# Attention scores of two heads issued in turns on the two halves of the rows, in a two-block sequence kernel on one Trainium2 core

## The chip, the cores and the metric

The kernel runs on one core of a Trainium2 chip. The metric is the time of one execution on the device in microseconds (us), as the median of several runs. The engines are named as the profile names them: PE is the matrix engine (TensorE) and PEld its weight loads, DVE is VectorE, ACT is ScalarE, POOL is GpSimd, SP is the engine that issues the loads from memory. PE writes its results into eight banks of PSUM, each of 128 partitions by 512 float32.

## What is computed

The reference is a chain of two blocks on 512 tokens of width 1024: a gated linear-attention layer, then a recurrent layer and an attention layer, each with feed-forward parts. The change lies in the attention layer alone, with 16 heads of width 64:

```python
def block(args):                       # one block of 128 queries
    qb, start = args
    z = jnp.einsum("bhqd,bhkd->bhqk", qb.astype(jnp.float32), k32) * scale
    q_pos = start + jnp.arange(Q_BLOCK)
    mask = key_pos[None, :] < q_pos[:, None]
    log_beta = jax.nn.log_sigmoid(z)
    log_1m = jnp.where(mask, jax.nn.log_sigmoid(-z), 0.0)
    suffix = lax.cumsum(log_1m, axis=3, reverse=True) - log_1m
    wts = jnp.where(mask, jnp.exp(log_beta + suffix), 0.0)
    return jnp.einsum("bhqk,bhkd->bhqd", wts, v32)
...
qkv = (h @ w_qkv.astype(h.dtype)).reshape(bsz, s, 3, SB_HEADS, SB_HEAD_DIM)
...
return o @ w_out.astype(h.dtype)
```

## The kernel before

All matrices are kept transposed (features on the partitions, tokens along the row). A float32 product is made of three products of rounded parts: every operand is split into a high and a low part (`...h`, `...l`), by a cast on ACT and a subtraction on DVE. Weights come from memory in slabs of 128 columns (`raw`), one load from SP each. `Feed` keeps the list of slabs in the order of their use; it splits each two products ahead (`whi`, L101 on ACT; `wlo`, L102 on DVE) into one of three slots.

The attention layer goes through eight passes `k`, each with two heads: head a lies on partitions 0 to 63 of the pass's q and k tiles, head b on partitions 64 to 127. The order of PE's instructions is the order in which the code is written (`manual_schedule`); those of the other engines are ordered by the framework. A pass has these steps:

- `proj`: the projections q, k and v of 24 products of 512 columns each (`psmm`, L173 to L175; for v they are named `psv` and come in two halves of 12). `evac` scales and splits the result: for q it is `qh` and `ql`, for k and v first `qk` (L1172).
- `scores(half, ...)`, L1119: twelve products of one head that contract 64 rows (`z`). Their widths are three times 512, 384, 128 and 256, since each of the four query blocks needs only its own and earlier keys; they fill three banks z0, z1, z2. Each bank then goes through eight sigmoids in all on ACT (`om`, `be`, L1124), masks on POOL (L1128), a scan on DVE (`pr`, L1131) and a product on DVE (`be`, L1134).
- `turn`, L1146: ten transposes of the weights `be` into three banks (t0, t1 and `nr`), and their split into w0, w1 and w2 (L1103, L1104).
- `vparts`, L1182: four transposes of v (`pv`) and their split (`vh`, `vl`).
- `values`, L1157: twelve products with v (`po`) of the same widths as the scores, and the split of the result (`Oh`, `Ol`, L1161 and L1162), the input of the output projection (`pso`, `out_part`).

PSUM's banks are shared out as two for projections, v's transposes and `po` (`mm`), three for the scores, two for the transposes, and one (`nr`) for the third group of the transposes.

Before, PE does in a pass: scores of head b, turn of a, projection k of the next pass, values of a, half of projection v, scores of head a of the next pass, turn of b, the other half of projection v, projection q of the pass after the next, values of b, and the transposes of v. So the scores of the two heads stand half a pass apart.

## Time and profile before

| what | value |
|---|---|
| median of three runs | 2080.22 us (2080.13 to 2083.77) |
| the profiled execution | 2082.17 us |
| its span | 2080.2 us |
| PE's busy share of the span | 99% |
| DVE, ACT, POOL | 53%, 37%, 12% |
| the eight attention passes | some 200 us from 1451 us on |

The profiled execution is 1.95 us above the median, and 1.97 us of it lie outside the span. The trace gives each instruction with its start and length. PE's instructions overlap: the length of a product contains its way through the array, so the rate is read from the distance of two starts, not from the length. "Idle" in brackets behind an instruction is the time in which its engine stood still before it, with the engine and the line that ended the wait.

### The profile page before, as it was taken

What the parts mean: (1) busy time and instruction counts of PE and PEld (TensorE: products, weight loads), DVE (VectorE), ACT (ScalarE), POOL (GpSimd) and SP (SyncE); (2) the same over time, 40 slices, a digit from 0 to 9 for tenths busy, and PEclk for the clock granted to TensorE, in tenths of its full rate; (3) what the DMA queues carried; (4) which work ended last, traced back from release to release, by engine and by line L of the source; (5) the groups of instructions that cost most, each with busy time, mean ns of one, the idle gap of its engine ahead of it and who ended that gap; (6) DMA issues with size and microseconds to landing.
All of it is one profiled execution on the core that took longest, in us unless ns stands there. A gap on an engine that the chain in (4) does not pass through costs nothing.

```text
span 2080.2 us, 24373 instructions
## 1 busy us (share of the span) xinstructions
PE 2051.9 (99%) x9786; PEld 1705.2 (82%) x9786; DVE 1104.5 (53%) x1455; ACT 763.9 (37%) x1099; POOL 257.1 (12%) x266
## 2 busy tenths in 40 slices
PE   8999999999999999999899999999999999999998
PEld 7778899888888888887788888888888888888887
DVE  5667453554444423669964444333877754444322
ACT  4334232333232322546642323223555533322221
POOL 0111000131000000252320000001322220000011
PEclk9999999999999999999999999999999999999999
DMA  4211111343333333322323333333122123333332
GB/s 168 71 55 59 60 41 43 105 127 101 97 96 100 91 97 98 114 79 82 91 91 96 97 101 92 92 101 98 55 61 72 41 77 96 91 102 94 92 102 68
DMA packets 53664, 181.69 MB, mean 87 GB/s; under 512 B 5808, under 2 KB 7984, under 8 KB 53552
## 3 DMA queue, kind: packets, MB, share of 16 engines
q1 hardware_dynamic: 53408, 180.05, 28.9%
q8 instruction: 76, 1.25, 0.3%
q14 instruction: 36, 0.29, 0.0%
q10 hardware_dynamic: 144, 0.10, 0.0%
HBM read 178.03 MB, written 2.10 MB: 87 GB/s over the span
## 4 chain that ended last, share of the span: by engine, by line
PE 91%; DVE 5%; ACT 1%; issue 1%; POOL 1%; DMA 1%; SPq 0%; POOLq 0%; DVEq 0%; ACTq 0%
PE psmm L173 19%; PE psmm L174 19%; PE psmm L175 19%; PE psd L173 6%; PE psd L175 6%; PE psd L174 6%; PE z L1119 2%; PE po L1157 1%; DVE wlo L102 1%; PE pU L731 1%; PE pX L726 1%; PE t L1146 1%; DVE xc L987 1%; PE psv L173 1%; PE psv L174 1%
## 5 line engine op out<-in xcount | busy, mean ns | idle before, releaser
L101 ACT CAST whi<-raw 128x1024 fp32r<-128x1024 f32 (+1 forms) x333 | 344.5, 1036 | 942.3 <-issue 374.5
L102 DVE TENSOR_TENSOR wlo<-raw,whi 128x1024 fp32r<-128x1024 f32 (+1 forms) x333 | 411.0, 1235 | 287.9 <-ACT whi L101 287.8
L173 PE MATMUL psmm<-Bh,wlo 128*128 128x512 f32 x1032 | 402.3, 390 | 0.3 <-DVE Ol L1162 0.3
L174 PE MATMUL psmm<-Bl,whi 128*128 128x512 f32 x1032 | 402.2, 390 | 0.1
L175 PE MATMUL psmm<-Bh,whi 128*128 128x512 f32 x1032 | 402.1, 390 | 0.0
L173 PE MATMUL psmm<-Ah,wlo 128*128 128x512 f32 x832 | 332.9, 401 | 2.8 <-DVE wlo L102 1.9
L175 PE MATMUL psmm<-Ah,whi 128*128 128x512 f32 x832 | 325.2, 391 | 0.0
L174 PE MATMUL psmm<-Al,whi 128*128 128x512 f32 x832 | 324.4, 390 | 0.6 <-DVE Al L189 0.6
L173 PEld LDWEIGHTS psmm<-Bh,wlo 128*128 128x128 f32 x1032 | 193.8, 188 | 40.8 <-DVE Ol L1162 0.5
L175 PEld LDWEIGHTS psmm<-Bh,whi 128*128 128x128 f32 x1032 | 193.8, 188 | 40.3
L174 PEld LDWEIGHTS psmm<-Bl,whi 128*128 128x128 f32 x1032 | 193.8, 188 | 40.2 <-DVE Bl L189 0.5
L216 POOL TENSOR_TENSOR ss<-ss,sq 128x512 f32<-128x512 f32 x55 | 85.6, 1561 | 1141.7 <-issue 803.7
L173 PE MATMUL psd<-Hh,wlo 128*128 128x512 f32 x506 | 196.8, 389 | 0.0
L174 PE MATMUL psd<-Hl,whi 128*128 128x512 f32 x506 | 196.8, 389 | 0.0
L175 PE MATMUL psd<-Hh,whi 128*128 128x512 f32 x506 | 196.8, 389 | 0.0
L173 PEld LDWEIGHTS psmm<-Ah,wlo 128*128 128x128 f32 x832 | 156.3, 188 | 36.0 <-DVE wlo L102 3.2
L175 PEld LDWEIGHTS psmm<-Ah,whi 128*128 128x128 f32 x832 | 156.1, 188 | 33.6
L174 PEld LDWEIGHTS psmm<-Al,whi 128*128 128x128 f32 x832 | 156.6, 188 | 30.3 <-DVE Al L189 1.1
L870 DVE TENSOR_TENSOR u<-psmm,R 128x512 f32<-128x512 f32 x66 | 45.6, 691 | 194.2 <-PE psmm L175 194.2
L866 DVE TENSOR_TENSOR s<-psmm,R 128x512 f32<-128x512 f32 x66 | 45.7, 692 | 137.0 <-PE psmm L175 134.0
L175 PEld LDWEIGHTS psd<-Hh,whi 128*128 128x128 f32 x506 | 95.0, 188 | 19.8
L174 PEld LDWEIGHTS psd<-Hl,whi 128*128 128x128 f32 x506 | 95.0, 188 | 19.8
(468 smaller groups left out, 2475.9 us busy)
## 6 DMA issues: line engine op xcount, KB each, us to landing
raw<-in_f SPq DMA_DIRECT2D x120, 512.0 KB, 3.6
raw<-in_w SPq DMA_DIRECT2D x60, 512.0 KB, 3.5
raw<-in_wA SPq DMA_DIRECT2D x43, 512.0 KB, 3.5
raw<-in_bQKV SPq DMA_DIRECT2D x24, 512.0 KB, 3.5
raw<-in_aIn SPq DMA_DIRECT2D x16, 512.0 KB, 3.6
raw<-in_f SPq DMA_DIRECT2D x16, 384.0 KB, 3.1
x<-in_xT SPq DMA_DIRECT2D x16, 256.0 KB, 3.6
raw<-in_wBr SPq DMA_DIRECT2D x8, 512.0 KB, 3.5
```

The source lines that it names most:

```text
L101: copied[0] = S.copy(hi[:, :nk, :], raw[:, :nk, :])
L102: V.tensor_tensor(lo[:, :nk, :], raw[:, :nk, :], hi[:, :nk, :].bitcast(F32), op=ALU.subtract)
L173: TE.matmul(ps, l, xh, start=(first and i == 0), stop=False)
L174: TE.matmul(ps, h, xl, start=False, stop=False)
L175: TE.matmul(ps, h, xh, start=False, stop=(last and i == n - 1))
L216: eng.tensor_tensor(self.acc, self.acc, sq, op=ALU.add)
L726: heads(lambda h: TE.matmul(pX[:, h], Nm[:, h, :], odd(U)[:, h], start=True, stop=True))
L731: heads(lambda h: TE.matmul(pU[:, h], Tt[:, h, :], X[:, h], start=True, stop=True))
L866: V.tensor_tensor(s1, p1, R, op=ALU.mult)
L870: V.tensor_tensor(u, p3, R, op=ALU.mult)
L987: V.scalar_tensor_tensor(ac, cx[:, j:j + T], col("aconv", 4 * k + j), ac, op0=ALU.mult, op1=ALU.add)
L1119: TE.matmul(zs[g][:, o:o + w], qp[a][qs], kp[b][p0:p0 + 64, 0:w], start=(n == 0 and o == 0), stop=(n == 2), skip_group_check=True)
```

## The change

`scores` now makes the products of both heads in one call: for every product of head a the same of head b follows at once, into a bank of its own. The sigmoids, masks, scans and products that stood in `scores` are now in `mix`, called once for each head. Each head has three banks (z00, z01, z02 and z10, z11, `nr`); the transposes of a head go into the banks of its scores, and its products with v into the third of these, which holds only 256 columns of scores. The two `mm` banks are left to the projections and v's transposes. In a pass PE now does: scores of both heads, projections q and k of the next pass, turn of a, half of projection v, turn of b, the other half, values of a, transposes of v, values of b. Before the first pass, v's transposes stand ahead of the scores. The list of slabs follows: q, k, v for each pass. The tiles of q and k have one buffer instead of two, those of w0, w1 and w2 two instead of one.

```diff
--- before.py
+++ after.py
@@ -159,9 +159,8 @@
     feed.add([aO[m] for m in range(KD)])
     feed.mark((0, 0, 1))
     ffn_plan(f13[0], f2[0])
-    feed.add([bQKV[8], bQKV[9], bQKV[0], bQKV[10]])
-    for k in range(KD - 1):
-        feed.add([bQKV[9 + 2 * (k + 1)], bQKV[k + 1]] + ([bQKV[8 + 2 * (k + 2)]] if k < KD - 2 else []))
+    for k in range(KD):
+        feed.add([bQKV[8 + 2 * k], bQKV[9 + 2 * k], bQKV[k]])
     feed.mark((2, 0, 0, 1))
     feed.add([bO[m] for m in range(KD)])
     feed.mark((0, 0, 1))
@@ -1104,20 +1103,29 @@
             V.tensor_tensor(lo[:, 0:w], src, hi[:, 0:w].bitcast(F32), op=ALU.subtract)
             return hi, lo
 
-        def scores(half, qp, kp):
-
-            p0 = 64 * half
-            zs = [psz.tile([P, T], F32, tag=f"z{g}", name=f"z{g}") for g in range(3)]
+        def bank(half, g, name):
+            if half and g == 2:
+                return pn.tile([P, T], F32, tag="nr", name=name)
+            return psz.tile([P, T], F32, tag=f"z{half}{g}", name=name)
+
+        def scores(qp, kp):
+
+
+            zs = [[bank(half, g, f"z{g}") for g in range(3)] for half in range(2)]
+            for g, i, o, w in QB:
+                for n, (a, b) in enumerate(((0, 1), (1, 0), (0, 0))):
+                    for half in range(2):
+                        p0 = 64 * half
+                        TE.matmul(zs[half][g][:, o:o + w], qp[a][p0:p0 + 64, i * P:(i + 1) * P], kp[b][p0:p0 + 64, 0:w],
+                                  start=(n == 0 and o == 0), stop=(n == 2), skip_group_check=True)
+            return zs
+
+        def mix(zs):
             be = SB.tile([P, 1280], F32, tag="be", bufs=2, name="be")
             om = SB.tile([P, 1280], F32, tag="om", bufs=2, name="om")
             pr = SB.tile([P, 1280], F32, tag="pr", bufs=1, name="pr")
             for g in range(3):
                 qbs = [(i, o, w) for g_, i, o, w in QB if g_ == g]
-                for i, o, w in qbs:
-                    qs = slice(p0, p0 + 64), slice(i * P, (i + 1) * P)
-                    for n, (a, b) in enumerate(((0, 1), (1, 0), (0, 0))):
-                        TE.matmul(zs[g][:, o:o + w], qp[a][qs], kp[b][p0:p0 + 64, 0:w], start=(n == 0 and o == 0),
-                                  stop=(n == 2), skip_group_check=True)
                 c0, cw = ZW[g]
                 for t, n in ((om, 1), (be, 0)):
                     for i, o, w in qbs:
@@ -1134,21 +1142,20 @@
                 V.tensor_tensor(be[:, c0:c0 + cw - 1], be[:, c0:c0 + cw - 1], pr[:, c0 + 1:c0 + cw], op=ALU.mult)
             return be
 
-        def turn(be):
+        def turn(half, be):
 
             out = []
             for g, (w, js) in enumerate(ZG):
-                t = pn.tile([P, T], F32, tag="nr", name="t2") if g == 2 else psz.tile([P, T], F32, tag=f"t{g}", name=f"t{g}")
+                t = bank(half, g, f"t{g}")
                 for j in js:
                     for i in range(j, NB):
                         c = next(ZW[g_][0] + o for g_, i_, o, _ in QB if i_ == i) + j * P
                         o = ZP[j][1] + (i - j) * P
                         TE.transpose(t[:, o:o + P], be[:, c:c + P], ident)
-                out.append(parts(f"w{g}", t[:, 0:w], w, 1))
+                out.append(parts(f"w{g}", t[:, 0:w], w, 2))
             return out
 
-        def values(k, half, wts, vp, pool=pmm, tag="mm"):
-            po = pool.tile([P, T], F32, tag=tag, name="po")
+        def values(k, half, wts, vp, po):
             n = 0
             for g in range(3):
                 for j in ZG[g][1]:
@@ -1167,10 +1174,10 @@
         def evac(ps, w):
 
             if w == 0:
-                return parts("q", ps, T, 2)
+                return parts("q", ps, T, 1)
             t = tp.tile([P, T], F32, tag="xin", bufs=3, name="qk")
             V.tensor_tensor(t, ps, R, op=ALU.mult)
-            return t if w == 2 else parts("k", t, T, 2)
+            return t if w == 2 else parts("k", t, T, 1)
 
         def proj(k, w):
 
@@ -1192,44 +1199,41 @@
             mm3(ps, [(hi[:, c, :], lo[:, c, :], O[c]) for c in ks], first=ks[0] == 0, last=ks[-1] == KD - 1)
 
         with tc.manual_schedule(engines={mybir.EngineType.PE}):
-            q, kk = proj(0, 0), proj(0, 1)
-            vt = proj(0, 2)
-            wa = scores(0, q, kk)
-            qn = proj(1, 0)
+            q, kk, vt = proj(0, 0), proj(0, 1), proj(0, 2)
             v = vparts(vt)
             for k in range(KD):
-                more = k < KD - 1
-                wb = scores(1, q, kk)
-                wt = turn(wa)
-                if more:
-                    kk, q = proj(k + 1, 1), qn
-                    values(k, 0, wt, v)
+                za, zb = scores(q, kk)
+                wa = mix(za)
+                if k < KD - 1:
+                    q = proj(k + 1, 0)
+                    wb = mix(zb)
+                    kk = proj(k + 1, 1)
+                    ta = turn(0, wa)
                     vhi, vlo = feed.next(bQKV[k + 1])
                     pv = pmm.tile([P, T], F32, tag="mm", name="psv")
                     mm3(pv, [(vhi[:, c, :], vlo[:, c, :], A[c]) for c in range(4)], last=False)
-                    wa = scores(0, q, kk)
-                    wt = turn(wb)
+                    tb = turn(1, wb)
                     mm3(pv, [(vhi[:, c, :], vlo[:, c, :], A[c]) for c in range(4, 8)], first=False)
                     vt = evac(pv, 2)
-                    if k < KD - 2:
-                        qn = proj(k + 2, 0)
-                    else:
-                        out_part(0, range(0, 6))
-                    values(k, 1, wt, v)
-                    v = vparts(vt)
+                    values(k, 0, ta, v, bank(0, 2, "po"))
+                    vn = vparts(vt)
+                    values(k, 1, tb, v, bank(1, 2, "po"))
+                    v = vn
                 else:
+                    out_part(0, range(0, 7))
+                    wb = mix(zb)
                     out_part(1, range(0, 7))
-                    values(k, 0, wt, v, psz, "z0")
-                    out_part(0, range(6, 7))
-                    wt = turn(wb)
-                    out_part(2, range(0, 7), psz, "z1")
-                    values(k, 1, wt, v, psz, "z0")
-            out_part(3, range(0, 7), psz, "z2")
+                    ta = turn(0, wa)
+                    tb = turn(1, wb)
+                    out_part(2, range(0, 7), psz, "z00")
+                    values(k, 0, ta, v, bank(0, 2, "po"))
+                    values(k, 1, tb, v, bank(1, 2, "po"))
+            out_part(3, range(0, 7), psz, "z01")
             for m in range(4):
                 out_part(m, range(7, 8))
         ss = SumSq("ss7")
         for m in range(KD):
-            ps = part[m][2] if m in part else gemm(psz, bO[m], O, tag=("z0", "t0", "t1", "z1")[m % 4])
+            ps = part[m][2] if m in part else gemm(psz, bO[m], O, tag=("z10", "z11", "z02", "z00")[m % 4])
             V.tensor_tensor(x_tiles[m], ps, x_tiles[m], op=ALU.add)
             split_scaled(A[m], x_tiles[m], col("nf1", m))
             ss.add(x_tiles[m])
```

Where the instructions stand is shown at three places. The first is PE's row at the change from the second pass to the third, before (z0 and z1 are the first two banks of one head's scores, `kl`, `kh`, `ql`, `qh` the parts of k and q):

```order
L1182 MATMUL pv_11177<-CST_76,qk_11125 128x128 x4
L1119 MATMUL z0_11186<-kl_11007,qh_10876 128x512
L1119 MATMUL z0_11186<-kh_11006,ql_10877 128x512
L1119 MATMUL z0_11186<-kh_11006,qh_10876 128x512
L1119 MATMUL z1_11187<-kl_11007,qh_10876 128x384
L1119 MATMUL z1_11187<-kh_11006,ql_10877 128x384
L1119 MATMUL z1_11187<-kh_11006,qh_10876 128x384
L1119 MATMUL z1_11187<-kl_11007,qh_10876 128x128
```

and after, at the same place (z0_11107 belongs to head a, z0_11110 to head b):

```order
L1164 MATMUL po_11092<-w2l_11051,vh_10806 128x256
L1164 MATMUL po_11092<-w2h_11050,vh_10806 128x256
L1119 MATMUL z0_11107<-kl_10982,qh_10915 128x512
L1119 MATMUL z0_11110<-kl_10982,qh_10915 128x512
L1119 MATMUL z0_11107<-kh_10981,ql_10916 128x512
L1119 MATMUL z0_11110<-kh_10981,ql_10916 128x512
L1119 MATMUL z0_11107<-kh_10981,qh_10915 128x512
L1119 MATMUL z0_11110<-kh_10981,qh_10915 128x512
L1119 MATMUL z1_11108<-kl_10982,qh_10915 128x384
```

The second head's products, which stood after a turn, projections and values, now follow those of the first one by one, and `values` (`po`) instead of v's transposes stand ahead of them.

The second place is DVE's row in the pass, before, from the scan of a head's first bank to the evacuation of q (`ql`):

```order
L1131 SCALAR_TENSOR_TENSOR pr_10767<-om_10766,anew_10420 128x512
L1134 TENSOR_TENSOR be_10765<-be_10765,pr_10767 128x511
L1131 SCALAR_TENSOR_TENSOR pr_10767<-om_10766,anew_10420 128x512
L1134 TENSOR_TENSOR be_10765<-be_10765,pr_10767 128x511
L1131 SCALAR_TENSOR_TENSOR pr_10767<-om_10766,anew_10420 128x256
L1104 TENSOR_TENSOR w0l_10812<-t0_10806,w0h_10811 128x512
L1134 TENSOR_TENSOR be_10765<-be_10765,pr_10767 128x255
L1104 TENSOR_TENSOR w1l_10821<-t1_10815,w1h_10820 128x512
L1104 TENSOR_TENSOR w2l_10828<-t2_10824,w2h_10827 128x256
L1172 TENSOR_TENSOR qk_10843<-psv_10749,R6_10393 128x512
L102 TENSOR_TENSOR wlo_10848<-raw_10743,whi_10847 128x1024
L1104 TENSOR_TENSOR ql_10877<-psmm_10851,qh_10876 128x512
```

and after, from the scans of the second head on (head a's three scans and products stand right ahead of these):

```order
L1139 SCALAR_TENSOR_TENSOR pr_10921<-om_10920,anew_10420 128x512 x2
L1139 SCALAR_TENSOR_TENSOR pr_10921<-om_10920,anew_10420 128x256
L1142 TENSOR_TENSOR be_10919<-be_10919,pr_10921 128x511
L1103 TENSOR_TENSOR ql_10916<-psmm_10890,qh_10915 128x512
L1142 TENSOR_TENSOR be_10919<-be_10919,pr_10921 128x511
L1142 TENSOR_TENSOR be_10919<-be_10919,pr_10921 128x255
L102 TENSOR_TENSOR wlo_10951<-raw_10884,whi_10950 128x1024
L1179 TENSOR_TENSOR qk_10979<-psmm_10954,R6_10393 128x512
L102 TENSOR_TENSOR wlo_11013<-raw_10948,whi_11012 128x1024
L1103 TENSOR_TENSOR w0l_10991<-t0_10985,w0h_10990 128x512
```

The evacuation of q now stands behind the scans of both heads, ahead of the split of the transposes of head a (`w0l`).

The third place is PE's row right after the first projection of v, before (the last rows of that projection, then head a's scores):

```order
L174 MATMUL psmm_10507<-Bl7_6306,whi_10431 128x512
L175 MATMUL psmm_10507<-Bh7_6305,whi_10431 128x512
L1119 MATMUL z0_10534<-kl_10498,qh_10460 128x512
L1119 MATMUL z0_10534<-kh_10497,ql_10461 128x512
L1119 MATMUL z0_10534<-kh_10497,qh_10460 128x512
```

and after:

```order
L173 MATMUL psmm_10507<-Bl7_6306,whi_10431 128x512
L174 MATMUL psmm_10507<-Bh7_6305,whi_10431 128x512
L1189 MATMUL pv_10534<-CST_76,qk_10532 128x128 x4
L1119 MATMUL z0_10543<-kl_10498,qh_10460 128x512
L1119 MATMUL z0_10546<-kl_10498,qh_10460 128x512
```

The transposes of v stand directly behind v's projection now.

## Rows read from the trace of the kernel before

**Rows 1.** The page, part 1: busy time, share of the span, instructions of each engine.

```profile
PE 2051.9 (99%) x9786; PEld 1705.2 (82%) x9786; DVE 1104.5 (53%) x1455; ACT 763.9 (37%) x1099; POOL 257.1 (12%) x266
```

**Rows 2.** Busy time by stretch: one whole pass. Columns: length, engines, PEclk, DMA.

```profile
1486.80:1514.23 27.43, 27.43 (x145) 23.26 (x145) 21.41 (x29) 15.31 (x31) 7.83 (x12) 1.00 0.20 58
```

**Rows 3.** Timeline of PE, one scores call. Columns: start us, length us, instruction.

```profile
1486.80 0.50 PE L1119 MATMUL z<-kl,qh 64*128 64x512 f32 x1
1487.14 0.40 PE L1119 MATMUL z<-kh,ql 64*128 64x512 f32 x1
1487.38 0.39 PE L1119 MATMUL z<-kh,qh 64*128 64x512 f32 x1
...
1488.93 1.31 PE L1146 MATMUL t<-CST,be 128*128 128x128 f32 x10
```

**Rows 4.** Timeline of PE: first and last of twelve products with v.

```profile
1495.58 0.39 PE L1157 MATMUL po<-w0h,vl 128*128 128x512 f32 x1
...
1497.37 0.28 PE L1157 MATMUL po<-w2h,vh 128*128 128x256 f32 x1
```

**Rows 5.** Timeline of PE: a scores call between plain products.

```profile
1450.62 0.39 PE L174 MATMUL psmm<-Bl,whi 128*128 128x512 f32 x1
1450.85 0.39 PE L175 MATMUL psmm<-Bh,whi 128*128 128x512 f32 x1
1451.17 0.49 PE L1119 MATMUL z<-kl,qh 64*128 64x512 f32 x1
...
1453.28 0.50 PE L173 MATMUL psmm<-Bh,wlo 128*128 128x512 f32 x1
1453.62 0.40 PE L174 MATMUL psmm<-Bl,whi 128*128 128x512 f32 x1
```

**Rows 6.** Timeline of weight loads (PEld) in the scores call of rows 3.

```profile
1488.15 0.18 PEld L1119 LDWEIGHTS z<-kh,ql 64*128 64x128 f32 x1
1488.26 0.19 PEld L1119 LDWEIGHTS z<-kh,qh 64*128 64x128 f32 x1
1488.37 0.19 PEld L1119 LDWEIGHTS z<-kl,qh 64*128 64x128 f32 x1
```

**Rows 7.** Timeline of ACT: first sigmoid and first cast after one head's eight sigmoids.

```profile
1487.87 0.69 ACT L1124 ACTIVATE om<-z,rq 128x512 f32<-128x512 f32 x1 [0.21 <-PE z L1119]
...
1491.16 0.64 ACT L1103 CAST w0h<-t 128x512 fp32r<-128x512 f32 x1
```

**Rows 8.** Timeline of DVE: the scans and products of one head.

```profile
1488.95 1.22 DVE L1131 TENSOR_TENSOR_SCAN pr<-om,anew 128x512 f32<-128x512 f32 x1 [0.15 <-POOL om L1128]
1490.30 0.88 DVE L1134 TENSOR_TENSOR be<-be,pr 128x511 f32<-128x511 f32 x1
1491.10 1.42 DVE L1131 TENSOR_TENSOR_SCAN pr<-om,anew 128x512 f32<-128x512 f32 x1
1492.62 0.78 DVE L1134 TENSOR_TENSOR be<-be,pr 128x511 f32<-128x511 f32 x1
1493.32 0.68 DVE L1131 TENSOR_TENSOR_SCAN pr<-om,anew 128x256 f32<-128x256 f32 x1
...
1494.51 0.41 DVE L1134 TENSOR_TENSOR be<-be,pr 128x255 f32<-128x255 f32 x1
```

**Rows 9.** Timeline of PE: its two waits from the sixth pass on, idle time in brackets.

```profile
1627.94 0.50 PE L173 MATMUL psmm<-Bh,wlo 128*128 128x512 f32 x1 [0.30 <-DVE Ol L1162]
...
1652.57 0.66 PE L1182 MATMUL pv<-CST,qk 128*128 128x128 f32 x4 [1.40 <-DVE Ol L1162]
```

**Rows 10.** Busy time by stretch, columns as in rows 2: after two waits.

```profile
1654.00:1660.00 6.00, 6.00 (x24) 5.48 (x23) 4.66 (x5) 4.80 (x11) 3.64 (x6) 0.50 0.00 0
1036.00:1042.00 6.00, 5.19 (x23) 3.86 (x21) 5.86 (x4) 1.25 (x2) 4.15 (x3) 1.00 0.18 73
```

**Rows 11.** Timeline of PE: an earlier wait, for comparison.

```profile
1034.50 0.50 PE L173 MATMUL psmm<-Ah,wlo 128*128 128x512 f32 x1 [1.60 <-DVE wlo L102]
```

**Rows 12.** Timeline of DVE: the first evacuation of v's projection.

```profile
1451.27 0.69 DVE L1172 TENSOR_TENSOR qk<-psmm,R 128x512 f32<-128x512 f32 x1 [0.52 <-PE psmm L175]
```

## The prediction

> **What bounds the kernel now.** The page's first part says that PE is busy for 99% of the span [rows 1], so PE's own time decides, and other engines count only where PE waits for them. The second view is one attention pass by stretches: of its 27.43 us PE is busy for all, DVE for 21.41, ACT for 15.31, POOL for 7.83, at a granted clock of 1.00 [rows 2]. So a pass is a full row of PE, and DVE with 78% is the next. The third view, PE's timeline, gives the rate: a score product of 512 columns starts 0.24 us after the one ahead of it [rows 3], a plain one 0.23 [rows 5], though the first contracts 64 rows and the second 128. Half of the array's rows are unused, for the price of the whole. The fourth view is what PE waited for: in the last passes 0.30 and 1.40 us, both for the split of a finished `po` that still held one of the two `mm` banks [rows 9]. After the second the clock is at 0.50, the lower of the two levels, for 6 us [rows 10].
>
> **Scores in turns.** A call's twelve products take 2.13 us beside transposes [rows 3]. The twelve products with v have the same widths and take 1.92 (1497.37 - 1495.58 and 0.13 for the last) [rows 4]. So a call is 1.92 of products and 0.21 of edges, and a pass holds two: 3.84 without edges. Now pairs of products use different rows and different banks. If they run at once, what limits the pair? Each brings its own weight load, and loads follow each other at 0.11 us in the narrow products [rows 6]. 24 loads at 0.11 are 2.64 per pass, a gain of 1.20. This I take: it is the nearest row, and for pairs of 512 columns two loads (0.22) are no longer than one product. Ends: 1.92 per pass if loads of different rows also overlap (gain 1.92), 3.84 if the products do not (gain 0). No row shows two products on different halves side by side. Eight passes give 9.6 us, between 0 and 15.4.
>
> The Trainium skill, in "TensorE: Matmul & The Clock Gate", section "Measured speedup vs the span model", counts a group of row tiles as one matmul plus about 4 ns for each further tile; by that rule the term would be the upper end, 15.4. No run here shows it yet.
>
> **The edges.** A call between plain products costs 0.39 beyond its twelve (1453.62 - 1450.85 less two plain starts of 0.23 and 1.92) [rows 5], one beside transposes 0.21 [rows 3]. Now one call of the first kind replaces two calls that touch transposes on a side, and the transposes get edges of their own. I count this as even; ends are 0.2 per pass either way, 1.6 us in all.
>
> **The waits that go.** `po` no longer takes an `mm` bank, and no output projection holds one in the seventh pass. So the waits of 0.30 and 1.40 go [rows 9], and with the latter the stretch at half clock: 6 us at 0.50 lose 3.0 us [rows 10], 3.2 with its ends. That is 4.9 us. What would be late next there is v's evacuation, below. A fall of the clock does not follow each wait (after 1.60 us at 1034 it stayed at 1.00 [rows 10, 11]), so I bind it to no length.
>
> **The waits that come.** First, v's transposes now stand right behind its first projection. The evacuation ends at 1451.27 + 0.69 = 1451.96 [rows 12], where PE had its next row from 1451.08 [rows 5]: 1.0 us, once, behind it all scores. Second, in the last pass two output parts (21 products of 0.23 each) stand between the scores and the turns; the turn of b is then reached 13.6 us after the pass's start by the working below, and b's last product, with no `ql` ahead of it, ends at 14.6: 1.0 us, once. Together 2.0 us.
>
> **Does a pass keep its pace?** This is the working for the cover of the other engines, from the start of the scores, t = 0. PE: scores to 2.9 (2.64 and edges), projections q and k to 13.8 (48 at 0.23, rounded down), turn of a to 14.9 (ten transposes, 1.31 us with the way of the last through the array [rows 3], 1.1 by starts), half of v to 17.7, turn of b to 18.8, the rest to 21.6, values to 23.6, v's transposes to 24.1, values to 26.1. ACT: its sigmoids begin at 1.07 (1487.87 - 1486.80) and take 3.29 per head [rows 3, 7]; for both heads, bank by bank, they end near 7.8. POOL's twelve masks take 7.83 [rows 2] and end near 10.4. DVE: one head's scans and products take 6.0 from 2.15 on [rows 8]; with the masks of both heads interleaved, head a is done near 9.3, needed at 13.8. Head b follows: scans of 1.45, 1.45 and 0.65, a product of 0.8, and then `ql` (0.69, as long as the evacuation in [rows 12]; 0.6 by starts) end near 14.1; the products of 0.8 and 0.35 end near 15.3. `ql` frees the bank of `psv`, wanted at 14.9: 0.8 us to spare. Head b is wanted at 17.7: 2.4 to spare. Behind come the splits for the turns, `qk` of v near 22.6 (wanted at 23.6), `Ol` of b near 27.6 (its bank is wanted by the next pass at 28.2). So nothing waits, with 0.6 to 1.0 us to spare at three places. The moved slabs cost nothing: three loads, casts and `wlo` per pass as before, two products ahead. DVE would be busy for 21.4 of some 26.2 us.
>
> **The sum.** -9.6 - 4.9 + 2.0 = -12.5 us. Against the profiled execution's 2082.17 that is 2069.7; the median of the runs is 1.95 lower, so 2067.7.
>
> **Rivals.**
>
> *Loads overlap too.* A pair costs one product, 1.92 per pass. For it: the two heads use separate rows for weights as for data. Against: the 0.11 us between loads is seen even where nothing else is in the way [rows 6]. It gives 5.8 us more: 2061.9. It is the case of the skill's page named above.
>
> *Pairs do not overlap.* The change then does not do what it says; the order alone changes. For it: no row of this trace shows an overlap. Against: the pairs share neither rows nor banks. It gives 9.6 us less gain: 2077.3, within 0.2%.
>
> *DVE's row becomes the bound.* Head b's scans and `ql` come in one row ahead of `psv` on DVE, and POOL's masks feed them. If masks of two heads delay head a's scans by 2.2 us more than I worked out, `psv` waits 1.4 us in each of seven passes; a wait of this size has halved the clock once here [rows 9, 10], at 3.2 us. Seven times 4.6 are 32 us on 2067.7: 2100, slower. It decides from a delay of 0.8 us on; below some 2 us it only eats the gain (1 us of wait in seven passes: 2075). For it: little to spare, and masks whose length is read roughly. Against: head a has 4.5 us to spare, and only `ql` is tight.
>
> The skill warns of this in "TensorEngine Tiling (Array Packing)", section "PSUM Bottleneck": tiles speed up the products, not the emptying of PSUM, which may become the limit. Here ACT and DVE had 12 and 6 us free in a pass, and by that the rival stays small.
>
> **How the numbers follow.** I give the forecast 0.47, overlapping loads 0.18, no overlap 0.20, the bound on DVE with a falling clock 0.10, and short waits in each pass 0.05. A difference of 0.2% (4.2 us) is about what a measurement of this kernel can tell from none: faster is below 2076.0, slower above 2084.4. Faster holds the first two and half of the last, 0.68; within 0.2% are no overlap and the other half, 0.22; slower 0.10. The range runs from the case of overlapping loads with even edges (2062, and 2 us for the edges) to that of no overlap with worse edges: 2060 to 2079. It leaves out the case on DVE and a little beyond each end.
>
> **What would show it.** After: one call of 24 `z` products of about 3.0 us per pass, pairs of 512 columns starting 0.23 us apart by the pair, a pass of about 26.2 us, no wait of v's transposes for `Ol` and no stretch at 0.50 near the end, a wait of about 1 us of `pv` near 1451. Starts of `z` 0.2 us apart for every product would say that nothing overlaps; waits of `psv` for `ql`, or of a turn for `be`, in every pass would say that DVE is the bound. The forecast is wrong if the call takes under 2.3 or over 3.6 us, or if such waits exceed 0.5 us per pass.

## The result and the profile after

The changed kernel takes 2061.38 us in the median (2061.19 to 2061.63, four runs), the kernel before 2080.43 us (2080.13 to 2083.77, four runs). The ratio is 0.9905, with a 95% interval from 0.9888 to 0.9922: faster by 0.8 to 1.1%. The forecast was 2067.7 us, its range 2060 to 2079. So the time lies inside the range, but at the place of a rival: 2061.9 us, "loads overlap too". The direction was right, and one term was too small.

The profiled execution took 2061.63 us, its span is 2059.9. The first part of the page answers to [rows 1]:

```profile
PE 2030.9 (99%) x9786; PEld 1688.0 (82%) x9786; DVE 1102.1 (54%) x1455; ACT 764.3 (37%) x1099; POOL 245.8 (12%) x266
```

The number of instructions is the same on every engine, PE is still busy for 99%, and it is busy for 21 us less. Busy time by stretch shows one attention pass and the stretch that was at half clock before (columns as in [rows 2]):

```profile
1503.84:1529.08 25.24, 25.24 (x146) 21.55 (x146) 20.90 (x28) 15.30 (x30) 6.45 (x12) 1.00 0.21 64
1654.00:1660.00 6.00, 6.00 (x28) 4.87 (x28) 0.71 (x2) 0.60 (x2) 0.00 (x0) 1.00 0.00 0
```

A pass takes 25.24 us where it took 27.43 [rows 2], and DVE is now busy for 83% of it. The stretch from 1654 to 1660 is at a clock of 1.00; in [rows 10] it was at 0.50. Next, PE's timeline through one scores call (start, length, instruction):

```profile
1503.84 0.50 PE L1119 MATMUL z<-kl,qh 64*128 64x512 f32 x2
1504.18 0.39 PE L1119 MATMUL z<-kh,ql 64*128 64x512 f32 x2
1504.41 0.39 PE L1119 MATMUL z<-kh,qh 64*128 64x512 f32 x2
1504.64 0.34 PE L1119 MATMUL z<-kl,qh 64*128 64x384 f32 x2
...
1505.75 0.28 PE L1119 MATMUL z<-kh,qh 64*128 64x256 f32 x2
1505.96 0.50 PE L172 MATMUL psmm<-Bh,wlo 128*128 128x512 f32 x1
```

Each row ends in x2: the two products of a pair start so close together that the view folds them into one row. The starts of the rows are 0.23 us apart at 512 columns, as those of single products were in [rows 3]. So 24 products take 2.12 us, one head's twelve took 2.13. And the weight loads of the same call (PEld) also come by twos:

```profile
1505.18 0.19 PEld L1119 LDWEIGHTS z<-kh,ql 64*128 64x128 f32 x2
1505.29 0.19 PEld L1119 LDWEIGHTS z<-kh,qh 64*128 64x128 f32 x2
```

In [rows 6] one load started every 0.11 us; here two do. What PE waited for in this stage (total, times, longest), from its first score to the output projection:

```profile
PE pv L1189 <- DVE qk L1179: 1.4, 2, 0.8
PE psmm L172 <- DVE wlo L102: 0.5, 1, 0.5
```

The two waits of `pv` are 0.78 us for v's first evacuation and 0.59 us in the sixth pass; the last one was there before too, with 0.60 us.

**Where the time went.** From the last product of the first projection of v to the output projection after the passes, the stage takes 210.95 us (1451.61 to 1662.56) and took 232.57 (1450.85 to 1683.42): 21.6 us less. Eight passes with 1.92 us less of products are 15.4; the rest of a pass's gain (27.43 - 25.23 = 2.20, less 1.92) is 0.28, eight times 2.2; the waits of 0.30 and 1.40 are gone, and so is the half clock, which in the kernel before lasts from 1653.5 to 1660.3 us, 6.8 us that cost 3.4: 5.1 together. Waits of 0.78 and 0.59 are new. That is 21.3. The rest of the program is 1.1 us longer in this execution than in that of before; no run shows why.

### The profile page after: what moved, and what is told of

It reads as the page before. It is cut to its first block, busy times and chain, and to the rows that moved or that the text cites. A ratio compares the mean times of both kernels' runs of the same rounds, so it can differ in the third digit from the quotient of the medians.

```text
span 2059.9 us, 24339 instructions
## 1 busy us (share of the span) xinstructions
PE 2030.9 (99%) x9786; PEld 1688.0 (82%) x9786; DVE 1102.1 (54%) x1455; ACT 764.3 (37%) x1099; POOL 245.8 (12%) x266
## 4 chain that ended last, share of the span: by engine, by line
PE 92%; DVE 5%; DMA 1%; ACT 1%; issue 1%; POOL 1%; SPq 0%; POOLq 0%; DVEq 0%
PE psmm L172 20%; PE psmm L173 19%; PE psmm L174 19%; PE psd L174 6%; PE psd L172 6%; PE psd L173 6%; PE po L1164 1%; DVE wlo L102 1%; PE pU L730 1%; PE pX L725 1%; DVE xc L986 1%; PE z L1119 1%; PE t L1154 1%; PE psS L591 1%; DMA raw<-in_aRI 1%
```

## Experiments

The first question was whether the pairs make the gain, the second what a pair costs, the third what each other part is worth. Two more ask how near DVE is, and whether the idea carries to other places. Times are medians; the ratios are to the kernel before, run beside them on the same chip (median 2081.25 for the first four, 2081.82 for the others). The changed kernel was not run again beside them, and the median of the kernel before moved by 0.8 and 1.4 us between these sets (2080.43 first), so a difference to the changed kernel's 2061.38 is good to about 1 us; the length of a pass in the trace is finer.

**One head after the other.** The alternation alone is undone:

```diff
-            for g, i, o, w in QB:
-                for n, (a, b) in enumerate(((0, 1), (1, 0), (0, 0))):
-                    for half in range(2):
+            for half in range(2):
+                for g, i, o, w in QB:
+                    for n, (a, b) in enumerate(((0, 1), (1, 0), (0, 0))):
```

> The changed kernel, with one thing undone: the 24 products of a scores call are issued head by head (twelve of head a, then twelve of head b), no longer in turns. Order of the work around, banks and waits stay. Theory (the gain of a pass is that a pair on the two halves costs one product): a call takes about 4.0 us for 2.1, only the last product of a and the first of b run together, so about 1.8 us more in each of eight passes, 14 to 15 us: 2075 to 2077. Rival (the gain is from the order and the waits that went, products of 64 rows run at their old rate in either kernel): no difference, 2061 to 2062.

Measured: 2072.68 us, ratio 0.9959 (0.9944 to 0.9974). The order alone does not make the gain, so the rival falls. But 11.3 us is less than the 14 to 15 expected, and PE's timeline shows why:

```profile
1507.54 0.27 PE L1119 MATMUL z<-kh,ql 64*128 64x128 f32 x1
1507.65 0.27 PE L1119 MATMUL z<-kh,qh 64*128 64x128 f32 x1
1507.65 0.50 PE L1119 MATMUL z<-kl,qh 64*128 64x512 f32 x2
1507.93 0.46 PE L1119 MATMUL z<-kh,ql 64*128 64x256 f32 x2
1508.05 0.58 PE L1119 MATMUL z<-kh,qh 64*128 64x256 f32 x2
1508.47 0.34 PE L1119 MATMUL z<-kl,qh 64*128 64x384 f32 x1
```

The second head's first three products (512 columns) run beside the first head's last three (256), though they stand behind them in the row; a folded row shows the shape of one of its two. From there on each product is alone again. So the call takes 3.64 us (1506.14 to 1509.78) and not 4.0, and a pass 26.77 instead of 25.23. This run also gives the edges by themselves: its pass is 0.66 us shorter than that of before, and its call 0.40 shorter than 24 single products with one pair of edges (3.84 + 0.20); 0.26 remain for the order, beside the 0.28 above.

**Turns after three products.**

```diff
             for g, i, o, w in QB:
-                for n, (a, b) in enumerate(((0, 1), (1, 0), (0, 0))):
-                    for half in range(2):
+                for half in range(2):
+                    for n, (a, b) in enumerate(((0, 1), (1, 0), (0, 0))):
```

> The changed kernel, but heads take turns after three products (the three that add up in one place of a bank), not after each. Theory (only products that are neighbours in PE's row run together): pairs form at the seven places where the half changes, four inside a width (0.21, 0.16, 0.05, 0.11 us) and three between widths (0.16, 0.05, 0.05), 0.8 of the 1.92 us that full turns save, so about 1.1 us more per pass and 9 us in all: 2070. Rival a (a half works through its products by itself, however they are queued): 2061 to 2062. Rival b (a pair must be issued product by product in matched widths, else nothing runs together): 2076 to 2077.

Measured: 2062.59 us, ratio 0.9912 (0.9896 to 0.9929): rival a. The products run in pairs as before, though three of one head stand ahead of three of the other:

```profile
L1119 PE MATMUL z<-kl,qh x4: 336/416/496, 1504.0 to 1504.8; 64*128 64x512 f32 x2, 64*128 64x384 f32 x2
```

(one line's products from 1504.0 to 1505.2: count, least, median and greatest length in ns, first and last start, forms). So my picture of the first run, neighbours only, was wrong: a half takes up its next products while the other half works on three that are queued ahead. With twelve ahead, only the last three ran beside the other head's. The call takes 2.13 us (1504.00 to 1506.12), so this order costs it nothing. The pass is 25.39 us all the same, 0.16 more than with full turns, and PE's timeline has that at another place, behind the turn of a:

```profile
1517.14 1.25 PE L1154 MATMUL t<-CST,be 128*128 128x128 f32 x10
1518.30 0.50 PE L172 MATMUL psv<-Bh,wlo 128*128 128x512 f32 x1
```

`psv` starts 1.16 us behind the turn's start, in the changed kernel 1.01 (1516.98 to 1517.99). In this run `ql`, which holds the bank that `psv` takes, stands on DVE behind all three products of head b and starts 13.55 us after the pass's start (1517.55), in the changed kernel behind the first of them, after 12.63 us (1516.47).

**The pair's price.** Every scores call is issued twice:

```diff
+            for _ in range(2):
                 for g, i, o, w in QB:
```

> The changed kernel with the 24 products of every scores call issued twice over, in turns (the second time they begin the sums anew, so the outputs stay). It prices the pair. Theory (a pair costs one product with its two weight loads): a call grows by twelve products, 1.92 us, eight times: 15.4 us, 2076.8. Rival a, the term on record (24 weight loads one after the other, 0.11 us each, limit the narrow pairs): 2.64 us a call, 21 us, 2082.5. Rival b (products of the two halves run one after the other): 3.84 us a call, 30.7 us, 2092.

Measured: 2076.65 us, 15.3 more than the changed kernel; the three theories stood at 15.4, 21 and 30.7. Its pass is 27.16 us, 1.93 more. A pair costs one product, weight loads included. PE's timeline at the seam, where no edge disturbs:

```profile
1509.82 0.28 PE L1120 MATMUL z<-kh,qh 64*128 64x256 f32 x2
1509.93 0.39 PE L1120 MATMUL z<-kl,qh 64*128 64x512 f32 x2
1510.17 0.40 PE L1120 MATMUL z<-kh,ql 64*128 64x512 f32 x2
```

**The bank alone, in the order of before.**

```diff
-                    values(k, 0, wt, v)
+                    values(k, 0, wt, v, pn, "nr")
...
-                    values(k, 1, wt, v)
+                    values(k, 1, wt, v, pn, "nr")
```

> The kernel before with one part of the change alone: the sums of the products with v of the first seven passes stand in the small bank of the third turn and no longer in one of the two mm banks. Order and scores as before. Theory (the two waits of 0.30 and 1.40 us in the seventh pass are for the split of these sums in an mm bank, and the half clock follows the second): the waits and the 6 us at half clock go, 4.6 to 4.9 us less than before, about 2075.7. Rival a (the waits go, the clock still falls there): 1.7 us less, 2078.7. Rival b (another wait takes their place in the seventh pass, the output part's bank or its slab): no difference, 2080.4.

Measured: 2082.23 us (2082.06 to 2082.61), ratio 1.0005 (0.9995 to 1.0014): no gain. The waits and the half clock went, as expected; busy time by stretch has the clock at 1.00:

```profile
1654.00:1660.00 6.00, 6.00 (x41) 5.34 (x41) 3.22 (x5) 3.62 (x8) 1.41 (x3) 1.00 0.28 90
```

But others came (PE's waits: total, times, longest):

```profile
PE po L1157 <- DVE w2l L1104: 3.1, 7, 1.4
PE t L1146 <- DVE Ol L1162: 0.3, 1, 0.3
```

The third turned piece stands in that bank until its split `w2l` is done, so now the first product with v waits for the last split; before, only its last three products needed it. It waits 0.17 us in most passes, and such a pass takes 27.87 us, 0.44 more than before. Five of these, the 0.90 of the first pass, and 0.34 and 1.39 in the seventh eat nearly all of what the two waits and the half clock had cost. The bank move pays only with the new order, which puts 2 us or more of other products between the turn and the products with v.

**The new order without the bank move.**

```diff
-                    values(k, 0, ta, v, bank(0, 2, "po"))
+                    values(k, 0, ta, v, pmm.tile([P, T], F32, tag="mm", name="po"))
                     vn = vparts(vt)
-                    values(k, 1, tb, v, bank(1, 2, "po"))
+                    values(k, 1, tb, v, pmm.tile([P, T], F32, tag="mm", name="po"))
```

> The changed kernel with its bank move undone: the sums of the products with v of the first seven passes stand in the two mm banks again. Theory (in this order, too, the mm banks are not free in time): the sums of b follow v's transposes by 0.5 us and take the bank of the sums of a, whose split ends 1.4 us after the last product of a (1526.62 and 1528.04 in the pass from 1503.84), so b waits about 0.9 us in each of seven passes, 6 us, 2067.7; if the clock falls after such a wait, up to 3 us more each time, 2090. Rival (the new order alone keeps these banks free): 2061 to 2062.

Measured: 2070.41 us, ratio 0.9948 (0.9933 to 0.9962), 9.0 us more than the changed kernel. The wait is there in each of seven passes, 0.95 us in six of them and 1.06 in the sixth, about as expected:

```profile
1502.40 0.60 PE L1189 MATMUL pv<-CST,qk 128*128 128x128 f32 x4
1503.96 0.50 PE L1164 MATMUL po<-w0h,vl 128*128 128x512 f32 x1 [0.95 <-DVE Ol L1169]
```

The clock stayed at 1.00 after all of them. But a pass is 1.22 us longer (26.45), not 0.95: PE had 0.60 us of transposes to finish before it stood idle, where without a wait the next product starts 0.36 us after `pv` (1526.62 to 1526.98 in the changed kernel). A wait costs its idle time and the overlap that it breaks, here 0.24 us by these starts and 0.27 by the pass.

**v behind the first scores, and a slab later.**

```diff
-            v = vparts(vt)
             for k in range(KD):
                 za, zb = scores(q, kk)
+                if k == 0:
+                    v = vparts(vt)
...
-    feed.mark((2, 0, 0, 1))
+    feed.mark((0, 0, 1, 2))
     feed.add([bO[m] for m in range(KD)])
```

> The changed kernel, with two edits: v's first transposes stand behind the first scores call (that part of the change undone), and the first slab of the output projection goes to a weight buffer that comes free a pass later, so its split does not stand in DVE's row of the sixth pass. Theory (the waits of 0.78 us at 1452.78 and of 0.59 us at 1603.07 are each whole on the path): both go, 1.4 us less, 2060.0. Rival (what the two products save is waited for later, for the next thing on DVE): 2061.4.

Measured: 2066.10 us, ratio 0.9931 (0.9914 to 0.9947): 4.7 us more, on neither theory's side. The 0.78 us went, and in the same pass PE stood for 4.60 us. DVE's row:

```profile
1460.47 0.51 DVE L1142 TENSOR_TENSOR be<-be,pr 128x255 f32<-128x255 f32 x1
1461.02 2.92 DVE L1139 TENSOR_TENSOR_SCAN pr<-om,anew 128x512 f32<-128x512 f32 x3
1463.85 0.67 DVE L1103 TENSOR_TENSOR vl<-pv,vh 128x512 fp32r<-128x512 f32 x1
```

PE's timeline (idle time in brackets), and behind it the busy time by stretch:

```profile
1464.57 0.80 PE L172 MATMUL psmm<-Bh,wlo 128*128 128x512 f32 x1 [4.60 <-DVE vl L1103]
```

```profile
1464.00:1470.00 6.00, 5.43 (x17) 4.38 (x18) 3.78 (x6) 0.00 (x0) 0.00 (x0) 0.72 0.20 53
```

The split `vl` of v now stands behind both heads' scans, and it holds the `mm` bank that the projection of k needs. After the wait the mean clock is 0.72 for 6 us, which is 1.7 us lost. So the early place of v's transposes is not a side effect: it costs 0.78 us once and spares 4.6 and a fall of the clock. The later slab moved the other wait from the sixth pass to the seventh, with 0.45 us for 0.59, so nothing much was won by it.

**How near DVE is.**

```diff
+                for _ in range(3 if g == 0 else 1):
                     V.tensor_tensor_scan(pr[:, sl][:, ::-1], om[:, sl][:, ::-1], anew[:, sl][:, ::-1], 1.0,
                                          op0=ALU.mult, op1=ALU.max)
```

> The changed kernel, but the first scan of each head (512 columns) runs three times, the same result each time: 2.3 us more on DVE per head, nothing on PE. It measures how near DVE's row is. Theory (0.8 us to spare ahead of ql, and 1.8 us of idle time inside head a that takes part of it): ql ends 2.9 us later, PE waits 2.1 us for the bank of psv in each of seven passes, 14.5 us, 2076; if the clock falls after each such wait, 3 us more each time, up to 2097. Rival a (DVE has room for all of it): 2061 to 2063. Rival b (nothing to spare): 4.7 us in each pass, 2094 and the clock besides.

Measured: 2087.73 us, ratio 1.0032 (1.0020 to 1.0044): 26.4 us more, slower than before. A pass takes 28.20 us, 2.97 more, for 4.7 us more work on DVE. PE's waits in the stage:

```profile
PE psv L172 <- DVE ql L1103: 9.5, 7, 1.4
PE t L1155 <- DVE be L1143: 7.8, 9, 2.4
PE pv L1190 <- DVE qk L1180: 4.2, 8, 1.5
```

`ql` is the first to be late, as worked out, but with 1.4 us, not 2.1; the turn of b (0.56) and `pv` (0.32, in the sixth pass 1.46) are late behind it in each of seven passes, which I had not counted, and three waits break the overlap three times. DVE then works for 25.48 of the pass's 28.20 us, and the clock is at 1.00 (columns as in [rows 2]):

```profile
1509.67:1537.87 28.20, 25.93 (x145) 21.58 (x145) 25.48 (x32) 15.30 (x30) 8.56 (x12) 1.00 0.18 55
```

In the last pass the turn of b is later still:

```profile
1667.42 0.77 PE L1155 MATMUL t<-CST,be 128*128 128x128 f32 x3 [2.37 <-DVE be L1143]
```

A second wait of 1.42 us follows 2 us later, and then the clock does fall: it is 0.72 in the mean from 1670 to 1676 us. The rival on DVE was the right next bound, with less room than "only `ql` is tight" said.

**The same pairing in the second mixer.** Its score products (plain f32) of two heads, one after the other into two banks, the row-decay sums then into the other ring:

```diff
+                pss = [pt("psS", shape=(P, T)) for _ in range(2)]
+                for hh in range(2):
+                    p0 = hh * 64
+                    TE.matmul(pss[hh][:, 0:w], mkT[hp // 2][p0:p0 + 64, j * P:(j + 1) * P], mqT[hp // 2][p0:p0 + 64, j * P:],
+                              start=True, stop=True)
...
+                    psr = pt("psr", "sb", (P, T))
```

> The changed kernel with the same idea at another place: the 16 score products of the second mixer (psS, 64 rows, plain f32, two runs over the columns each, 1.05 us for 512 columns), whose heads also lie on the two halves of the rows, are issued in pairs. Both banks of their ring are taken by a pair, so the row-decay sums take the other ring. Theory (f32 products on the two halves run together as well): 10.6 us of products become 5.3, 2056. Rival a (f32 products with their longer weight loads, 0.18 us twice, do not run together): 2061 to 2062. Rival b (the second ring is not free in time, PE waits at the row-decay sums or at the transposes that use it): above 2062.

Measured: 2054.33 us, ratio 0.9874 (0.9859 to 0.9888), 7.0 us less than the changed kernel. PE's timeline, first the changed kernel's single product, then the pair:

```profile
97.35 1.12 PE L591 MATMUL psS<-x,x 64*128 64x512 f32 x2
98.40 0.49 PE L595 MATMUL psr<-rjl,sel 4*128 4x512 f32 x1
```

```profile
121.59 1.13 PE L592 MATMUL psS<-x,x 64*128 64x512 f32 x4
122.65 0.49 PE L598 MATMUL psr<-rjl,sel 4*128 4x512 f32 x1
```

Two products in two runs each (x4) take 1.06 us, one took 1.05 (x2). By their starts the sixteen products took 11.73 us and take 6.91 as eight pairs, 4.8 us less where 5.3 were expected: the first pair ran as two singles, because the weight load of its second product waited 0.70 us for ACT.

```profile
70.03 2.12 PE L592 MATMUL psS<-x,x 64*128 64x512 f32 x4
```

The other 2.2 us lie outside these products. PE's row changes from 128 rows to 64 and back at eight places fewer, but the edit also moves the work that fills PE's row between them, and no run parts the two.

**The products with v in pairs, on halves of the columns.** Each head needs 64 of v's 128 columns, and used to multiply with all of them, three times in split parts:

```diff
-                    for (a, b) in ((1, 0), (0, 1), (0, 0)):
-                        TE.matmul(po[:, j * P:], vp[a][:, j, :], wts[g][b][:, o:o + NW[j]], start=(n == 0), stop=(n == 11),
+                    for half in range(2):
+                        s_ = slice(64 * half, 64 * half + 64)
+                        TE.matmul(po[half][s_, j * P:], vp[:, j, s_], wts[half][g][:, o:o + NW[j]],
+                                  start=(n == 0), stop=(n == 3), skip_group_check=True)
```

> The changed kernel, with the products with v paired too, on the two halves of the array's columns (each head uses 64 of the 128 columns of v that it multiplied with until now), and in plain f32, in one product where there were three of split parts; the splits of the turned rows and of v become plain copies. Rows: a plain f32 product of 512 columns takes 1.05 us, its pair on the halves of the rows 1.06, so 1280 columns take 2.6 us a pair where 24 products took 3.84. Theory (halves of the columns run together as halves of the rows do): 1.2 us less in each of eight passes, about 9 us less with an edge or two for the change of form, 2052. Rival a (no overlap on the columns: 5.25 us a pass): 1.4 us more, 2072. Rival b (the products now need the turn of b as well, 2 us earlier than before; PE waits for its copies): 2061 and more.

Measured: 2050.07 us, ratio 0.9847 (0.9833 to 0.9862), 11.3 us less than the changed kernel, 2 us better than the theory. PE's timeline of all products with v of one pass:

```profile
1498.14 1.08 PE L1174 MATMUL po<-w0h,vh 128*64 128x512 f32 x4
1499.05 1.03 PE L1174 MATMUL po<-w1h,vh 128*64 128x384 f32 x8
1499.91 0.60 PE L1174 MATMUL po<-w2h,vh 128*64 128x256 f32 x4
1500.44 0.66 PE L1200 MATMUL pv<-CST,qk 128*128 128x128 f32 x4
```

Busy time by stretch, one pass:

```profile
1501.03:1524.88 23.85, 23.85 (x137) 18.81 (x136) 18.44 (x23) 14.36 (x29) 6.42 (x12) 1.00 0.22 67
```

2.30 us replace twice 1.92; halves of the columns run side by side too. The pass takes 23.85 us, and DVE is relieved by 2.5 us of it, since the turned rows need no split. The wait of the sixth pass is gone as well. The run changes two things at once, the pairing and the three products that became one. That the halves run together is read from the time: at 1.05 us for 512 columns, the two heads one after the other would take some 5.2 us (an estimate), not 2.30.

**Both pairings.**

> Both pairings together: the score products of the second mixer (7.1 us less by themselves, 2054.3) and the products with v (as expected above). The two lie in different stages, so their gains should add: 2061.4 less 7.1 less the gain of the products with v by themselves, 2045 if that is 9.

Measured: 2043.86 us (2042.72 to 2046.89), ratio 0.9823 (0.9806 to 0.9839). The gains add: 2061.4 less 7.0 less 11.3 is 2043.1. This version beats both kernels, by 38 and 17.5 us.

## Why the prediction was right, and where it was not

**What bounds the kernel** held: PE was the bound, DVE the next, and the experiment with more scans showed it.

**Scores in turns** is the step that failed, by its size: 9.6 us were 15.4. I took the spacing of weight loads on single products, 0.11 us [rows 6], as the rate at which a pair is fed. Those loads all went to the same half of the rows, so the row says nothing on two halves; the trace after shows two loads in 0.11 us, and issuing the call twice prices the pair at one product to within 0.01 us a call. The rule of the Trainium skill's page "TensorE: Matmul & The Clock Gate", section "Measured speedup vs the span model", was the better guide: a group of tiles counted as one matmul and about 4 ns for each further tile, measured there with tiles of 32 rows or columns. The trace agrees with it, 24 products in 2.12 us. The call also stayed below the 2.3 us that the prediction gave as its own limit.

**The edges**, the time lost where PE goes from 128 rows to 64 and back or to transposes, were taken as even with 1.6 us either way and gave 2.2 us (0.28 a pass; 0.26 by the run with one head after the other). By the starts in a pass, two scores calls took 4.25 us from their starts to what follows them, the one now takes 2.12: one such edge of 0.21 is gone. The transposes went from 2.13 to 2.02 us and those of v from 0.53 to 0.36, and the products with v ahead of the call take 0.19 us more. So the transposes did not get the dearer edges that I had set against the saved call.

**The waits that go** went, with the stretch at half clock: 5.1 us for 4.9 worked out, since the half clock lasted 6.8 us and not 6. But the bank move does not do it alone: in the order of before it gains nothing, and the new order without it loses 9.0 us.

**The waits that come** were half right. v's first transposes waited 0.78 us for 1.0. The turn of b in the last pass does not wait; the scores call was 0.8 us shorter than worked out, and DVE's row earlier by as much or more. Not foreseen were the 0.59 us of the sixth pass. There, the split of the first output slab (`wlo`) stands ahead of b's splits and of v's evacuation `qk`:

```profile
1599.66 1.22 DVE L102 TENSOR_TENSOR wlo<-raw,whi 128x1024 fp32r<-128x1024 f32 x1 [0.86 <-ACT whi L101]
1600.80 0.68 DVE L1103 TENSOR_TENSOR w0l<-t,w0h 128x512 fp32r<-128x512 f32 x1
...
1602.33 0.68 DVE L1179 TENSOR_TENSOR qk<-psv,R 128x512 f32<-128x512 f32 x1
```

I had counted three slabs in every pass; the sixth has a fourth, because its weight buffer was free all along.

**Does a pass keep its pace?** It did. Head a was done 9.1 us after the pass's start (9.3 worked out) and head b near 14.3 (15.3). DVE's row in the pass from 1503.84:

```profile
1512.39 0.51 DVE L1142 TENSOR_TENSOR be<-be,pr 128x255 f32<-128x255 f32 x1
...
1516.47 0.69 DVE L1103 TENSOR_TENSOR ql<-psmm,qh 128x512 fp32r<-128x512 f32 x1
1517.08 1.02 DVE L1142 TENSOR_TENSOR be<-be,pr 128x511 f32<-128x511 f32 x2
```

`ql` ends near 1517.1 and `psv` starts at 1517.99: 0.8 us to spare, as worked out.

**The sum.** Against the stage's gain, 12.5 us were predicted and 21.6 came: 5.8 from the pairs, 2.2 from the edges, 0.6 from new waits, 0.2 from the half clock, 0.3 that I cannot place. Of these 9.1 us the rest of the program took back 1.1, and 1.7 is a matter of the reference: the profiled execution of before lay 1.95 us above the median of its runs, that of after 0.25. That leaves the 6.3 us between forecast and median. Whether the half clock falls in each of before's runs is open; their spread of 3.6 us against 0.6 in the run with the bank alone, where it did not fall, makes it doubtful. The mean clocks of these runs do not settle it: at 0.997 the spans are 2078.9 to 2079.2 us, at 0.995 2078.0 to 2081.0.

**The rivals.** "Loads overlap too" was given 0.18 and is what happened. It deserved more: the row against it came from a case without two halves, and a stated rule spoke for it. That its time, 2061.9 us, came within 0.5 us is in part luck: the stage gained 3.3 us more than this rival's 18.3, and the rest of the program and the reference took 2.8 of them back. "Pairs do not overlap" fell. The bound on DVE did not come; it is 0.8 us away, and less than that when `ql` falls later in DVE's row, as in the run with turns after three products.

## What to carry to other kernels

Where two products contract 64 rows each (or fill 64 columns each), issue them near each other on the two halves, into different banks: here a pair cost one product, in three places and two number formats, and the gains of the places added. Both products must be free to start: the one pair whose second product had to wait ran as two singles. Price such a pair from rows in which two halves are at work, not from the spacing on one half. Move banks and order together: a bank is only worth what the order lets it be free, and a split that holds a bank must stand early in its engine's row.

## What had not been expected of the hardware

- A half does not need strict turns. Three products of one half ahead of three of the other cost the call nothing (2.13 us for 2.12); with twelve ahead of twelve, three still ran beside the other half. Products of two halves then do not start in the order of PE's row: the second head's first starts at 1507.65 us, 0.1 us ahead of the first of three that stand before it.
- Weight loads of two halves start together, two in 0.11 us.
- Plain f32 products, with two runs over the columns, pair up as well (1.06 us for two, 1.05 for one), and so do halves of the columns (2.30 us for 16 instructions that cover 1280 columns of each head).
- A wait of PE cost 0.22 to 0.27 us beyond its idle time: 1.22 for 0.95, 0.44 for 0.17, and 0.81 for the 0.59 of the changed kernel's sixth pass (26.04 us for 25.23).
- The clock stayed at 1.00 through seven waits of 0.95 to 1.06 us, and through three waits in each of seven passes (1.38, 0.56 and 0.32 in most); it fell after 4.60 us (mean 0.72 over 6 us), after 2.37 and 1.42 us close together (0.72), and in the kernel before after 1.40 [rows 10].
- The length of one wait did not decide it. The wait of [rows 11] is in every trace, at code that no edit touches: after 1.80 us in the run with turns after three the mean clock was 0.72 from 1036 to 1042 us, after 2.83 us in the changed kernel it was 1.00.
